# A decoder block on one core: first-stage elementwise work off GpSimd, merge products read from the bank, and new places for merge steps and last scalings

## The chip, the cores and the metric

The kernel runs on one core of a Trainium2 chip. A core has a matrix engine (TensorE; PE for matmuls, PEld for weight loads), VectorE (DVE), ScalarE (ACT), GpSimd (POOL) and SyncE (SP, which here only issues DMAs). Each engine works through its own instruction list in order and waits on semaphores. Matmul results land in eight PSUM banks of 128 x 512 float32, which DVE and ACT can read. The metric is the device time of one execution in microseconds (us), the median of three runs.

## The reference, cut to what matters

One layer, 1024 positions, width 1024, all float32:

```
h = rmsnorm(x);  z = h @ w_in;  gates = sigmoid(h @ w_gate + b_gate)     # 3 x 1024 gate columns
y_a = u * (chunked causal mix of layernorm(v))     # u, v = gelu of the first 512 columns of z
y_b = causal mean pooling (windows 2,4,8,16) of 256 columns, @ pool_w, * pool_scale
y_c = differential attention, 4 heads: softmax(q1 k1 + bias) - lam * softmax(q2 k2 + bias), @ v; rmsnorm per head
merged = g_a*(y_a @ proj_a) + g_b*(y_b @ proj_b) + g_c*(y_c @ proj_c)
x = x + merged @ w_out
x = x + (gelu(causal_conv(gate)) * up) @ w_down    # gate, up = rmsnorm(x) @ w_up, 2816 columns each
out = rmsnorm(x)
```

## The kernel before, in words

Activations are held transposed, features on the 128 partitions, eight tiles of 128 x 1024; j = 0, 1 are the two halves of 512 positions. Every float32 product is made of three matmuls of a rounded high part and a low remainder: ACT casts the high part, another engine subtracts it from the source to get the low part (the `split` lines, L96 and L97; L316 and L317 for h). The large products use a seven-product Strassen-like scheme (L189 holds all matmuls of it; `b` is a bank, T/S/A are combined operands).

**First stage** (to about 75 us). For j = 0 and then j = 1: x tiles are loaded, `scaled` makes the split h blocks (hb), 48 matmuls fill two banks `pu` (the u columns) and `v_part` two more per half (the v columns). `squares` (L330 on POOL for even tiles, L332 on ACT for odd) and the additions of L336 sum x² over the tiles; `factors` (L339 to L344) turns the sum into 1/rms, written to `R8` (R in the trace). `bcast_rows` (L146, L148) multiplies R into an identity on PE to spread it over partitions, and ACT copies the bank to `RB`, by which u is multiplied. After each half, `v_gelu` (L427) reads the v banks. `winograd` (L207 to L212) forms in place the combinations of x for the scheme, for tiles 0, 2 and 3 on POOL and for tile 1 on DVE. `load_V` loads the value weights in small parts through a pool of six half-size buffers (`wr`, in_w_tm) and splits them.

**Middle.** Values, the pooled columns (`pooling`, L542 to L551, woven into the first q/k product; `pool_out`, L576, its small product), q/k and 12 pairs of gate products; gates go to DRAM (g_d). `start` (L827, L830) copies a bank to an x tile with the residual added by DMA.

**Attention and merge** (about 460 to 660 us). 32 tiles of 128 queries run as a software pipeline over steps t. In a step, `scores` computes q k for the two softmaxes: chunk by chunk of up to 512 columns PE fills a bank, DVE adds the bias and takes the minimum of the negated scores in the same instruction (L675), a small DVE reduction joins the two chunks (L681), ACT takes the exponential (L683). `combine` (L1000 to L1002, DVE) subtracts the two softmaxes; `transpose` (PE L1017, ACT copy L1018) and `attend` (PE L1026, one bank) give the head's output, copied by ACT (L1029), whose squares DVE sums from SBUF (L1032). `sub_norm` (L1044 to L1056) normalizes a head. Between these pieces a generator `filler = merge_ab()` is advanced once per step: six matmuls into one of two `mm` banks, an ACT copy `pc` (L1096), a POOL multiplication by the gate tile (L1097), and after each fourth step a POOL addition of the b part to the a part (L1099). `load_p` loads and splits w_proj (low part on POOL for a/b, on DVE for c). `merge_c` multiplies the c part on DVE (L1122) and adds it to the same tile by an accumulating DMA issued from POOL (L104).

**End.** The last half of the last product is made in two quarters q (`tail2`): sums of squares on PE (L1287), 1/rms (`finish`, L1294 and L123 to L131), spreading (L1300), a copy to RB (L1303), and `scale_out` of four output pairs k: POOL after an ACT multiplication (L1251, L1252) or DVE in one instruction (L1254).

A scheduler orders the instructions of each engine from the program's order and its priorities; `tc.high_priority()` asks it to place what stands inside early. Buffers come from pools and are reused in order.

Of the kernel before, what the change touches and what calls it, by code (L numbers as in the profile page):

```python
# [15 lines left out]
ALU = mybir.AluOpType  # L16
# [31 lines left out]
def trunk_kernel(  # L48
# [147 lines left out]
    class Act:  # L196
# [2 lines left out]
            self.T = [{} for _ in range(4)]  # L199


        def winograd(self, xt, j, T4=True, eng=None):

            t, u = xt[j], xt[j + 4]
            b11, b12, b21, b22 = t[:, :NH], t[:, NH:], u[:, :NH], u[:, NH:]
            e = eng or nc.gpsimd
            e.tensor_tensor(out=b11, in0=b12, in1=b11, op=ALU.subtract)  # L207
            e.tensor_tensor(out=b12, in0=b22, in1=b12, op=ALU.subtract)
            e.tensor_tensor(out=b22, in0=b22, in1=b11, op=ALU.subtract)
            t1, t3 = op2(t, a4, "T")  # L210
            if T4:
                e.tensor_tensor(out=b21, in0=b21, in1=b22, op=ALU.subtract)  # L212
                t4, t2 = op2(u, a4, "T")
                self.T[j].update(T4=t4)
            else:
                t2 = op1(b22, "T2")
            self.T[j].update(T1=t1, T2=t2, T3=t3)
# [106 lines left out]
    def squares(kt, j):  # L324

        k = 2 * j + kt % 2
        src = xt[kt][:, half(j)]
        sq = c2("acc" if kt < 2 else "sq")
        if kt % 2 == 0:
            nc.gpsimd.tensor_tensor(out=sq, in0=src, in1=src, op=ALU.mult)  # L330
        else:
            nc.scalar.activation(out=sq, in_=src, func=AF.Square)  # L332
        if kt < 2:
            acc[k] = sq
        else:
            (nc.gpsimd, nc.vector)[kt % 2].tensor_tensor(out=acc[k], in0=acc[k], in1=sq, op=ALU.add)  # L336

    def factors(j):
        nc.vector.tensor_tensor(out=acc[2 * j], in0=acc[2 * j], in1=acc[2 * j + 1], op=ALU.add)  # L339
        ps = pm1()  # L340
        ss_cols(ps, acc[2 * j], 4, 1, 0)
        t = tiny(4, "ssum")
        nc.vector.tensor_scalar(out=t, in0=ps[:, :4], scalar1=1.0 / D, scalar2=1e-6, op0=ALU.mult, op1=ALU.add)
        nc.vector.tensor_copy(R8[:, 4 * j:4 * j + 4], rsqrt(t, 4, j == 0))  # L344

    def gain(kt):
        nc.scalar.mul(xt[kt], xt[kt], col(C_GA + kt))
# [87 lines left out]
    for j in range(2):  # L435
        pu = [pb1() for _ in range(2)]
        for kt in range(KT):
            if j == 0 and kt in (1, 2, 3):
                for g in gens:
                    next(g)  # L440
            if j == 0 and kt in (1, 3):
                for k in range(kt + 1, kt + 3):
                    load_x(k, 0)
                if kt == 3:
                    load_x(6, 0)
                    load_x(7, 0)
            if j == 0 and kt == 3:
                w_v = [next(load_parts(w_tm[0, k].rearrange("p a b -> p (a b)"), 1)) for k in range(2)]
            if j == 0 and kt == 5:
                for k in range(KT):  # L450
                    load_x(k, 1)
            if j == 0:
                scaled(kt, j)
            for i in range(2):
                mm3(pu[i], wsl(w_u[i], kt), h.b[kt][j], kt == 0, kt == KT - 1)
            if j == 1:
                squares(kt, 1)
        if j == 0:
            pv = [v_part(0, 0, lambda k: squares(k, 0))]
            factors(0)  # L460
            for kt in range(KT):
                scaled(kt, 1)
            pv.append(v_part(0, 1))
        else:
            w_V = [load_V(c) for c in range(2)]
            wk, wsm, pbd = load_wide()
            rel_bias()
            factors(1)
            pv = [v_part(1, 0)]
        bcast_rows(R8[:, 4 * j:4 * j + 4], 4, RB[:, half(j)], pm1)  # L470
        u_gelu(j, pu)
        if j == 1:
            pv.append(v_part(1, 1))
        for g in range(2):
            v_gelu(j, g, pv[g])
# [106 lines left out]
    h.winograd(xt, 0)  # L582
    layer_norm()
    values(1, (2, 3))
    h.winograd(xt, 1, eng=nc.vector)
    values(0, (0, 1))
    h.winograd(xt, 2)
    gating(0)
# [25 lines left out]
        store_qk(i, strassen_pair(ops, h, pb1, lambda: next(pl, None)))  # L614
    for _ in pl:
        pass
    for f in range(2):
        pool_out(f, zb[f])

    def load_head(hd):  # L620

# [30 lines left out]
    def scores(t, c):  # L652

        if t >= len(tiles):
            return
        hd, i = tiles[t]
        H = heads[hd]
        W = (i + 1) * P
        if c == 0:
            if W <= NH:  # L660
                b = a4([P, 2, NH], n="sc")
                st[t] = dict(pr=[b[:, 0, :], b[:, 1, :]], s=[])
            else:
                st[t] = dict(pr=[a4(n="sc"), a4(n="sc")], s=[])
        q, kh, kl = H["qkl"][c]
        sc_ = st[t]["pr"][c]
        mx = tiny(2, "mx")
        chunks = [(0, min(NH, W))] + ([(NH, W - NH)] if W > NH else [])
        for n_, (c0, n) in enumerate(chunks):
            ps = score_bank[0]()  # L670
            qs = q[:, i * P:(i + 1) * P]
            nc.tensor.matmul(ps[:, :n], lhsT=qs, rhs=kh[:, c0:c0 + n], start=True, stop=False)
            nc.tensor.matmul(ps[:, :n], lhsT=qs, rhs=kl[:, c0:c0 + n], start=False, stop=True)
            o = (7 - i) * P + c0
            nc.vector.tensor_tensor_reduce(  # L675
                out=sc_[:, c0:c0 + n], in0=ps[:, :n], in1=H["T"][:, o:o + n], scale=1.0, scalar=3.0e38,
                op0=ALU.add, op1=ALU.min, accum_out=mx[:, n_:n_ + 1])
        nm_ = mx[:, 0:1]
        if len(chunks) > 1:
            nm_ = tiny(1, "nmx")  # L680
            nc.vector.tensor_reduce(out=nm_, in_=mx, axis=AX.X, op=ALU.min)  # L681
        sum_ = H["s0"][:, i:i + 1] if c == 0 else tiny(1, "s1")
        nc.scalar.activation(out=sc_[:, :W], in_=sc_[:, :W], func=AF.Exp, bias=nm_, scale=-1.0, accum_out=sum_)  # L683
        st[t]["s"].append(sum_)

    for n_ in range(12):
        Fs = strassen_pair(w_gate[n_], h, pb1)
        for k, F in enumerate(Fs):
            m = 2 * n_ + k
            times_r(F)  # L690
            nc.scalar.activation(out=F, in_=F, func=AF.Sigmoid, bias=col(C_BG + m), scale=1.0)
            nc.sync.dma_start(out=g_d[m], in_=F)
# [31 lines left out]
    def strassen_full(src, w, nsl, x_d, out, done, tail=None, LL=4):  # L724
# [113 lines left out]
        def after(p):  # L838
            R4 = range(4)
            if p == 0:  # L840
                for d in R4:
                    later(1, start, d, 0, B[0][d])
            if p == 1:
                for d in R4:
                    plus(d, 0, B[1][d])
                for d in R4:
                    fin(d, 0, 3)
            if p == 2:
                for d in R4:
                    start(d, 1, B[0][d])  # L850
                for d in R4:
                    later(3, start, 4 + d, 1, B[2][d])
            if p == 3:
                for d in R4:
                    start(4 + d, 0, B[0][d])
                    later(4, plus, 4 + d, 1, B[0][d])
                for d in R4:
                    fin(4 + d, 1, 5)
            if p == 5:
                for d in R4:  # L860
                    plus(d, 1, B[2][d])
                    fin(d, 1, 5)
# [157 lines left out]
    def attend(t):  # L1020
# [4 lines left out]
        for kb in range(i + 1):  # L1025
            nc.tensor.matmul(po[:, :P], lhsT=AH[t][:, kb, :], rhs=H["V"][:, kb, :], start=kb == 0, stop=kb == i)  # L1026
            if kb % 4 == 3:
                yield
        nc.scalar.copy(H["O"][:, i, :], po[:, :P])  # L1029
        junk = c2("sq")  # L1030
        o = H["O"][:, i, :]
        nc.vector.tensor_tensor_reduce(out=junk[:, :P], in0=o, in1=o, scale=1.0, scalar=0.0, op0=ALU.mult,  # L1032
                                       op1=ALU.add, accum_out=H["ss"][:, i:i + 1])
        yield

    ycv = [[None, None] for _ in range(NHEAD)]
# [20 lines left out]
            ycv[hd][j] = op_g(pt, col(C_SG), "yc")  # L1057
            yield

    def load_p(m, g, eng=nc.gpsimd):  # L1060
        raw = c2(n="pr")
        nc.sync.dma_start(out=raw, in_=w_proj[m, :, 4 * g:4 * g + 4, :].rearrange("p a b -> p (a b)"))
        hl = w4([P, 2, NH], F32R, "ph")
# [21 lines left out]
    def merge_ab():  # L1085
        for m in range(KT):
            ga, gb, whl = ab(m)
            for j in range(2):
                if j == 1 and m < KT - 1:
                    ab(m + 1)  # L1090
                for g, k in ((ga, 0), (gb, 2)):
                    ps = pmm()
                    for ki in range(2):
                        mm3(ps, wsl(whl, k + ki), yab[k + ki][j], ki == 0, ki == 1)
                    t = c2("pc")
                    nc.scalar.copy(t, ps)  # L1096
                    nc.gpsimd.tensor_tensor(out=g[:, half(j)], in0=t, in1=g[:, half(j)], op=ALU.mult)  # L1097
                    if (g, j) == (gb, 1):
                        nc.gpsimd.tensor_tensor(out=ga, in0=ga, in1=gb, op=ALU.add)  # L1099
                        mg.append(ga)  # L1100
                    yield

# [27 lines left out]
    for t in range(len(tiles) + 3):  # L1130
# [10 lines left out]
            scores(t, 0)  # L1141
        transpose(t - 2, 0)
        next(avs, None)
        if t >= 1:
            next(filler, None)
        scores(t, 1)
        combine(t - 1)
# [9 lines left out]
            avs = attend(t - 2)  # L1157
        if lates and next(lates[0], 0) == 0:
            lates.pop(0)
        if t >= 29:  # L1160
            pre_c(t - 29)
        if t >= 34:
            next(mc)
    for _ in avs:
        pass
# [110 lines left out]
    def tail2(hold):  # L1276
# [13 lines left out]
        def finish(q):  # L1290
# [11 lines left out]
            sl = slice(q * n, (q + 1) * n)  # L1302
            nc.scalar.copy(RB[:, sl], pb[:, :n])  # L1303
            for k in range(4):
                scale_out(k, 0, sl, RB[:, sl], nc.gpsimd if k <= (2, 0)[q] else nc.vector)
            yield

        pend, fins = None, iter(())
# [143 lines left out]
```

## Time and profile before

| what | us |
|---|---|
| median of three runs (1421.44 to 1428.28) | 1421.71 |
| the profiled execution | 1421.06 |
| its span, first to last instruction | 1419.4 |
| PE busy | 1355.5 (96 %) |
| DVE busy | 984.9 (69 %) |
| ACT busy | 652.4 (46 %) |
| POOL busy | 621.7 (44 %) |

Busy time of PE is an upper measure, since matmuls are pipelined and their ends are modelled. [...]

### The profile page before, as it was taken

To read this page: it belongs to the slowest core of one execution; us is meant where nothing else is said; L and a number is where in the kernel's file an instruction comes from. 1 tells how busy PE (TensorE), PEld (TensorE's weight loads), DVE (VectorE), ACT (ScalarE), POOL (GpSimd) and SP (SyncE) were. 2 spreads that over 40 slices of the span, in tenths; PEclk is the share of its full clock that TensorE was granted. 3 is DMA by queue.
4 is the path that set the end of the run, shared out by engine and by line. 5 is a ranking of instruction groups with operands and counts; after the bars stand their busy time and mean duration, and the time that the engine had idled before them with its cause. 6 is when DMAs were issued, how large, how long until landed. Compare 5 with 4: busy or idle time off the path is not lost. (4 is left out here: it accounts for less than half of the span.)

```text
span 1419.4 us, 17845 instructions
## 1 busy us (share of the span) xinstructions
PE 1355.5 (96%) x6502; PEld 1130.4 (80%) x6502; DVE 984.9 (69%) x1502; ACT 652.4 (46%) x1065; POOL 621.7 (44%) x399
## 2 busy tenths in 40 slices
PE   7799999999999889989989999999999999999996
PEld 6699777888888677778868788888888887888786
DVE  8764676454444889976959766677676668985854
ACT  6442244443434666642567433343434335455461
POOL 6523365555544545442132466666666640102014
PEclk9999999999999999999999999999999999999998
DMA  5232044323336986358796122222222247945753
GB/s 188 96 112 90 30 178 151 132 104 119 120 118 173 287 223 185 105 185 191 185 245 159 52 102 77 90 89 74 90 89 74 75 144 273 305 128 151 215 127 119
DMA packets 78256, 200.46 MB, mean 141 GB/s; under 512 B 8206, under 2 KB 17550, under 8 KB 78168
## 3 DMA queue, kind: packets, MB, share of 16 engines
q1 hardware_dynamic: 67800, 180.44, 38.6%
q0 software_dynamic: 10368, 18.88, 7.9%
q8 instruction: 51, 0.84, 0.2%
q14 instruction: 37, 0.30, 0.1%
HBM read 143.70 MB, written 47.46 MB: 135 GB/s over the span
## 5 line engine op out<-in xcount | busy, mean ns | idle before, releaser
L189 PE MATMUL b<-ft,fw 128*128 128x512 f32 (+1 forms) x1308 | 291.7, 383 | 8.3 <-ACT ft L96 3.1
L189 PEld LDWEIGHTS b<-ft,fw 128*128 128x128 f32 x1308 | 238.9, 188 | 58.3 <-ACT ft L96 3.9
L351 POOL TENSOR_TENSOR F<-F,RB 128x1024 f32<-128x1024 f32 x74 | 206.0, 2785 | 145.9 <-DVE F L260 135.4
L189 PE MATMUL b<-hb,Ah 128*128 128x512 f32 x608 | 190.1, 392 | 0.0
L260 DVE TENSOR_TENSOR F<-b,c 128x512 f32<-128x512 f32 x152 | 100.8, 683 | 112.8 <-ACT c L279 68.7
L189 PE MATMUL b<-T,Sh 128*128 128x512 f32 x504 | 155.7, 389 | 1.9 <-ACT c L270 1.9
L232 POOL TENSOR_TENSOR s<-r 128x512 f32<-128x512 f32 x36 | 57.0, 1584 | 200.8 <-DMA r<-in_w_up 96.6
L189 PEld LDWEIGHTS b<-hb,Ah 128*128 128x128 f32 x608 | 114.5, 189 | 24.6 <-issue 1.0
L97 DVE TENSOR_TENSOR Sl<-s,Sh 128x1024 fp32r<-128x1024 f32 x76 | 114.0, 1500 | 26.2 <-PE b L189 22.1
L97 DVE TENSOR_TENSOR Al<-r,Ah 128x1024 fp32r<-128x1024 f32 x38 | 52.6, 1385 | 98.2 <-issue 77.7
L189 PE MATMUL b<-hb,Al 128*128 128x512 f32 x304 | 119.0, 392 | 0.8 <-DVE Al L97 0.8
L96 ACT CAST Sh<-s 128x1024 fp32r<-128x1024 f32 x76 | 80.0, 1052 | 72.8 <-PE b L189 48.6
L189 PEld LDWEIGHTS b<-T,Sh 128*128 128x128 f32 x504 | 94.6, 188 | 21.9 <-ACT c L270 2.4
L189 PE MATMUL b<-hb,Sh 128*128 128x512 f32 x304 | 95.4, 396 | 3.9 <-DVE F L260 3.9
L189 PE MATMUL b<-T,Sl 128*128 128x512 f32 x252 | 98.1, 389 | 0.0
L96 ACT CAST Ah<-r 128x1024 fp32r<-128x1024 f32 x38 | 40.0, 1053 | 110.4 <-PE b L189 106.7
L96 ACT CAST fw<-fr 128x512 fp32r<-128x512 f32 x90 | 54.7, 622 | 64.9 <-DVE fw L97 29.0
L189 PE MATMUL b<-Tl,Sh 128*128 128x512 f32 x204 | 79.4, 389 | 0.0
L189 PE MATMUL b<-Th,Sh 128*128 128x512 f32 x204 | 78.7, 390 | 0.7 <-ACT c L270 0.7
L189 PE MATMUL b<-Th,Sl 128*128 128x512 f32 x204 | 78.6, 389 | 0.0
L104 POOL DMA_DIRECT2D ssb<-sq x24 | 20.7, 876 | 125.8 <-ACT sq L171 37.8
L97 DVE TENSOR_TENSOR A<-r,A 128x512 fp32r<-128x512 f32 x38 | 74.6, 1964 | 0.9 <-ACT A L96 0.9
(260 smaller groups left out, 2982.8 us busy)
## 6 DMA issues: line engine op xcount, KB each, us to landing
fr<-in_w_down SPq DMA_DIRECT2D x47, 512.0 KB, 4.6
r<-in_w_up SPq DMA_DIRECT2D x42, 512.0 KB, 3.5
r<-in_w_gate SPq DMA_DIRECT2D x24, 512.0 KB, 4.1
g_d<-F SPq DMA_DIRECT2D x24, 512.0 KB, 4.8
act_d<-cv SPq DMA_DIRECT2D x22, 512.0 KB, 2.6
act<-act_d SPq DMA_DIRECT2D x22, 512.0 KB, 6.8
fr<-in_w_out SPq DMA_DIRECT2D x18, 512.0 KB, 4.0
ssb<-sq POOLq DMA_DIRECT2D x24, 256.0 KB, 3.9
```

Of the source, the lines that this page charges most:

```text
L96: nc.scalar.copy(hi, src)
L97: (eng or nc.vector).tensor_tensor(out=lo, in0=src, in1=hi.bitcast(F32), op=ALU.subtract)
L104: nc.gpsimd.dma_start(out=dst, in_=src, accum_op=ALU.add)
L189: nc.tensor.matmul(ps, lhsT=w[a], rhs=x[b], start=first and i == 0, stop=last and i == 2, skip_group_check=more)
L232: eng.tensor_tensor(out=s1[:, :NH], in0=a21, in1=a22, op=ALU.add)
L260: nc.vector.tensor_tensor(out=o, in0=ps, in1=c, op=ALU.add)
L351: (eng or nc.gpsimd).tensor_tensor(out=F, in0=F, in1=RB, op=ALU.mult)
```

## The change: what it does

- First stage: all squares go to ACT, all additions of squares and all of `winograd` to DVE; `factors` and the spreading of R stand under `high_priority`.
- `pool_out` is no longer called behind the q/k products but handed, through a generator, to the first gate products.
- `scores`: the second chunk's instruction takes the first chunk's minimum as its start value, so the reduction L681 goes.
- `attend`: the squares are taken on ACT from the bank, summed by the same instruction.
- `load_p` puts the low part on DVE for a/b too; in `merge_ab` DVE multiplies the bank by the gate tile in one instruction, and the addition of b to a becomes an accumulating DMA.
- The filler is left out at t = 10, 18, 26 and advanced twice from t = 32; `pre_c` and the advance of `merge_c` begin one step earlier.
- `start(d, 1, ...)` of the output products stands under `high_priority`.
- End: in quarter 0 POOL scales all four pairs; in quarter 1 POOL scales k = 0 and DVE scales the others with the bank itself as second input.

```
-        if kt % 2 == 0:
-            nc.gpsimd.tensor_tensor(out=sq, in0=src, in1=src, op=ALU.mult)
-        else:
-            nc.scalar.activation(out=sq, in_=src, func=AF.Square)
+        nc.scalar.activation(out=sq, in_=src, func=AF.Square)
...
-            (nc.gpsimd, nc.vector)[kt % 2].tensor_tensor(out=acc[k], in0=acc[k], in1=sq, op=ALU.add)
+            nc.vector.tensor_tensor(out=acc[k], in0=acc[k], in1=sq, op=ALU.add)
...
-        bcast_rows(R8[:, 4 * j:4 * j + 4], 4, RB[:, half(j)], pm1)
+        with tc.high_priority():
+            bcast_rows(R8[:, 4 * j:4 * j + 4], 4, RB[:, half(j)], pm1)
...
-                out=sc_[:, c0:c0 + n], in0=ps[:, :n], in1=H["T"][:, o:o + n], scale=1.0, scalar=3.0e38,
+                out=sc_[:, c0:c0 + n], in0=ps[:, :n], in1=H["T"][:, o:o + n], scale=1.0,
+                scalar=mx[:, 0:1] if n_ else 3.0e38,
...
-        nc.vector.tensor_tensor_reduce(out=junk[:, :P], in0=o, in1=o, scale=1.0, scalar=0.0, op0=ALU.mult,
-                                       op1=ALU.add, accum_out=H["ss"][:, i:i + 1])
+        nc.scalar.activation(out=junk[:, :P], in_=po[:, :P], func=AF.Square, accum_out=H["ss"][:, i:i + 1])
...
-                    t = c2("pc")
-                    nc.scalar.copy(t, ps)
-                    nc.gpsimd.tensor_tensor(out=g[:, half(j)], in0=t, in1=g[:, half(j)], op=ALU.mult)
+                    nc.vector.tensor_tensor(out=g[:, half(j)], in0=ps, in1=g[:, half(j)], op=ALU.mult)
                     if (g, j) == (gb, 1):
-                        nc.gpsimd.tensor_tensor(out=ga, in0=ga, in1=gb, op=ALU.add)
+                        accumulate(ga, gb)
...
-        if t >= 1:
+        if t >= 1 and t not in (10, 18, 26):
+            next(filler, None)
+        if t >= 32:
             next(filler, None)
...
-                scale_out(k, 0, sl, RB[:, sl], nc.gpsimd if k <= (2, 0)[q] else nc.vector)
+                if q == 0 or k == 0:
+                    scale_out(k, 0, sl, RB[:, sl], nc.gpsimd)
+                else:
+                    scale_out(k, 0, sl, pb[:, :n], nc.vector)
```

How the instructions move, at two places. First, DVE in the first stage, where R of the half j = 0 is finished: rs and ssum are the 128 x 4 values of the 1/rms computation, wl the low parts of the value weights, x the tiles that `winograd` combines. Before:

```order
37 L124 RECIPROCAL rs_48_326<-rs_49_327 128x4
38 L339 TENSOR_TENSOR acc_429<-acc_429,acc_437 128x512
39 L129 SCALAR_TENSOR_TENSOR rs_49_327<-rs_48_326 128x4
40 L130 TENSOR_TENSOR rs_49_327<-rs_49_327,ssum_324 128x4
41 L131 SCALAR_TENSOR_TENSOR rs_48_326<-rs_49_327,rs_48_326 128x4
42 L344 COPY R_93<-rs_48_326 128x4
43 L208 TENSOR_TENSOR x_86<-x_90,x_86 128x512
44 L97 TENSOR_TENSOR wl_494<-wr_495,wh_493 128x512
```

And in the changed kernel, from the third of these small instructions on:

```order
58 L131 SCALAR_TENSOR_TENSOR rs_48_326<-rs_49_327,rs_48_326 128x4
59 L97 TENSOR_TENSOR wl_494<-wr_499,wh_493 128x512
60 L209 TENSOR_TENSOR x_91<-x_91,x_87 128x512
61 L97 TENSOR_TENSOR wl_504<-wr_505,wh_503 128x512
62 L212 TENSOR_TENSOR x_90<-x_90 128x512
63 L97 TENSOR_TENSOR wl_504<-wr_509,wh_503 128x512
64 L209 TENSOR_TENSOR x_92<-x_92,x_88 128x512
65 L342 COPY R_93<-rs_48_326 128x4
```

The copy to R moves from row 42 to row 65, behind three splits of the value weights and most of the `winograd` instructions.

Second, PE at the same time: m_407 is the bank in which R is spread, b_421 and b_422 are the pu banks of j = 1, b_590 is the first v bank of j = 1. Before:

```order
159 L189 MATMUL b_421<-hb_343,wh_109 128x512 x2
160 L189 MATMUL b_421<-hb_343,wl_110 128x512
161 L189 MATMUL b_422<-hb_343,wh_115 128x512
162 L146 MATMUL m_407<-ident,R_93 128x128 x4
163 L189 MATMUL b_422<-hb_343,wh_115 128x512
164 L189 MATMUL b_422<-hb_343,wl_116 128x512
```

In the changed kernel:

```order
175 L189 MATMUL b_421<-hb_355,wh_109 128x512 x2
176 L189 MATMUL b_421<-hb_355,wl_110 128x512
177 L189 MATMUL b_422<-hb_355,wh_115 128x512 x2
178 L189 MATMUL b_422<-hb_355,wl_116 128x512
179 L146 MATMUL m_407<-ident,R_93 128x128 x4
180 L385 MATMUL m_547<-oh_544,rb 4x512
181 L189 MATMUL b_590<-wh_183,hb_334 128x256
```

The spreading of R now stands behind the last pu matmul (of hb_355, the eighth tile) and no longer behind those of the fourth tile (hb_343).

## Rows read from the trace of the kernel before

**Rows 1.** Busy time in stretches; PE, PEld, DVE, ACT, POOL (x instructions), PEclk, DMA share, GB/s.

```profile
0.00:20.00 20.00, 12.29 (x44) 8.82 (x45) 13.37 (x16) 15.19 (x28) 11.41 (x15) 0.88 0.85 290
...
40.00:60.00 20.00, 12.82 (x51) 10.47 (x50) 19.84 (x24) 8.45 (x14) 12.41 (x9) 0.83 0.31 103
...
460.00:500.00 40.00, 34.90 (x188) 28.22 (x187) 31.41 (x87) 25.26 (x55) 19.38 (x11) 0.96 0.97 280
500.00:540.00 40.00, 36.41 (x223) 31.97 (x222) 34.41 (x116) 26.38 (x68) 18.61 (x12) 0.96 0.77 214
540.00:580.00 40.00, 37.42 (x233) 31.93 (x233) 37.31 (x133) 28.29 (x72) 18.87 (x14) 1.00 0.62 172
580.00:635.00 55.00, 45.95 (x265) 38.86 (x264) 44.95 (x139) 31.36 (x79) 24.03 (x17) 0.94 0.43 137
```

**Rows 2.** PE in the first stage, in order of time: start, duration, instruction, idle before.

```profile
18.27 0.79 PE L189 MATMUL b<-hb,wh 128*128 128x512 f32 x1 [4.67 <-DVE hb L317]
51.19 2.05 PE L146 MATMUL m<-ident,R 128*128 128x128 f32 x8 [7.18 <-DVE R L344]
61.54 0.38 PE L189 MATMUL b<-wh,hb 128*128 128x256 f32 x1
```

**Rows 3.** DVE, then ACT, in the first stage, in order of time.

```profile
24.05 0.68 DVE L336 TENSOR_TENSOR acc<-acc,sq 128x512 f32<-128x512 f32 x1
...
44.28 0.17 DVE L124 RECIPROCAL rs<-rs 128x4 f32<-128x4 f32 x1
...
49.85 1.19 DVE L344 COPY R<-rs 128x4 f32<-128x4 f32 x1
...
55.97 0.62 ACT L96 CAST wh<-wr 128x512 fp32r<-128x512 f32 x1 [6.63 <-DMA wr<-in_w_tm]
57.09 1.28 ACT L427 ACT_TABLE_LOAD   x1
58.39 1.57 ACT L427 ACTIVATE vg<-b,R 128x256 f32<-128x256 f32 x4
```

**Rows 4.** PE at the small pooling product, in order of time.

```profile
167.69 2.81 PE L576 MATMUL m<-F,wpp 128*128 128x512 f32 x4 [2.61 <-issue]
```

**Rows 5.** What PE waited for, 460 to 635 us: total us, times, longest.

```profile
PE sc L672 <- DVE mx L675: 5.5, 4, 2.6
...
PE b L189 <- DVE F L260: 1.4, 1, 1.4
```

**Rows 6.** Groups of DVE and ACT instructions, 460 to 640 us: busy, mean ns, idle before.

```profile
L1032 DVE CUSTOM_DVE_ANT_0 sq<-O 128x128 f32<-128x128 f32 x32 | 17.0, 533 | 5.3 <-ACT O L1029 5.3
L1001 DVE SCALAR_TENSOR_TENSOR nr<-nr,s,nlam 128x1 f32<-128x1 f32 x32 | 12.8, 401 | 0.6
L1002 DVE SCALAR_TENSOR_TENSOR sc<-sc,nr,sc 128x896 f32<-128x896 f32 x4 | 6.6, 1646 | 0.1
L681 DVE TENSOR_REDUCE nmx<-mx 128x1 f32<-128x2 f32 x32 | 4.7, 148 | 0.1
...
L1096 ACT COPY pc<-mm 128x512 f32<-128x512 f32 x32 | 18.4, 583 | 3.9 <-PE mm L189 3.9
```

**Rows 7.** DVE and POOL at two places of the attention, in order of time.

```profile
590.16 1.15 DVE L1002 SCALAR_TENSOR_TENSOR sc<-sc,nr,sc 128x896 f32<-128x896 f32 x1
...
615.31 1.24 DVE L1044 TENSOR_TENSOR e<-s 128x4 f32<-128x4 f32 x1
...
615.14 1.39 POOL L1097 TENSOR_TENSOR gb<-pc,gb 128x512 f32<-128x512 f32 x1 [3.14 <-ACT pc L1096]
```

**Rows 8.** The page: a group of DVE instructions that read a bank.

```profile
L260 DVE TENSOR_TENSOR F<-b,c 128x512 f32<-128x512 f32 x152 | 100.8, 683 | 112.8 <-ACT c L279 68.7
```

**Rows 9.** The page: accumulating DMAs issued from POOL, KB each, us to landing.

```profile
ssb<-sq POOLq DMA_DIRECT2D x24, 256.0 KB, 3.9
```

**Rows 10.** DVE at the end, in order of time.

```profile
1406.58 0.41 DVE L1324 TENSOR_TENSOR x<-b,x 128x256 f32<-128x256 f32 x1
...
1412.05 3.49 DVE L1254 SCALAR_TENSOR_TENSOR x<-x,cs,RB 128x256 f32<-128x256 f32 x6 [1.72 <-ACT RB L1303]
```

More of the change, by code (lines that the diff above doesn't have):

```diff
@@ L199, in __init__, with winograd @@
             self.T = [{} for _ in range(4)]
-        def winograd(self, xt, j, T4=True, eng=None):
+        def winograd(self, xt, j, T4=True):
             t, u = xt[j], xt[j + 4]
             b11, b12, b21, b22 = t[:, :NH], t[:, NH:], u[:, :NH], u[:, NH:]
-            e = eng or nc.gpsimd
+            e = nc.vector
             e.tensor_tensor(out=b11, in0=b12, in1=b11, op=ALU.subtract)
@@ L335, in squares @@
         else:
-            (nc.gpsimd, nc.vector)[kt % 2].tensor_tensor(out=acc[k], in0=acc[k], in1=sq, op=ALU.add)
+            nc.vector.tensor_tensor(out=acc[k], in0=acc[k], in1=sq, op=ALU.add)
     def factors(j):
[L339 to L344, printed above, removed]
+        with tc.high_priority():
+            nc.vector.tensor_tensor(out=acc[2 * j], in0=acc[2 * j], in1=acc[2 * j + 1], op=ALU.add)
+            ps = pm1()
+            ss_cols(ps, acc[2 * j], 4, 1, 0)
+            t = tiny(4, "ssum")
+            nc.vector.tensor_scalar(out=t, in0=ps[:, :4], scalar1=1.0 / D, scalar2=1e-6, op0=ALU.mult, op1=ALU.add)
+            nc.vector.tensor_copy(R8[:, 4 * j:4 * j + 4], rsqrt(t, 4, j == 0))
     def gain(kt):
@@ L469, in trunk_kernel @@
             pv = [v_part(1, 0)]
-        bcast_rows(R8[:, 4 * j:4 * j + 4], 4, RB[:, half(j)], pm1)
+        with tc.high_priority():
+            bcast_rows(R8[:, 4 * j:4 * j + 4], 4, RB[:, half(j)], pm1)
         u_gelu(j, pu)
@@ L584, in trunk_kernel @@
     values(1, (2, 3))
-    h.winograd(xt, 1, eng=nc.vector)
+    h.winograd(xt, 1)
     values(0, (0, 1))
@@ L616, in trunk_kernel, with pool_outs @@
         pass
-    for f in range(2):
-        pool_out(f, zb[f])
+    def pool_outs():
+        for f in range(2):
+            for _ in range(2):
+                yield
+            pool_out(f, zb[f])
+    po_ = pool_outs()
     def load_head(hd):
@@ L675, in scores @@
             nc.vector.tensor_tensor_reduce(
-                out=sc_[:, c0:c0 + n], in0=ps[:, :n], in1=H["T"][:, o:o + n], scale=1.0, scalar=3.0e38,
+                out=sc_[:, c0:c0 + n], in0=ps[:, :n], in1=H["T"][:, o:o + n], scale=1.0,
+                scalar=mx[:, 0:1] if n_ else 3.0e38,
                 op0=ALU.add, op1=ALU.min, accum_out=mx[:, n_:n_ + 1])
[L678 to L681, printed above, removed]
+        nm_ = mx[:, n_:n_ + 1]
         sum_ = H["s0"][:, i:i + 1] if c == 0 else tiny(1, "s1")
@@ L686, in trunk_kernel @@
     for n_ in range(12):
-        Fs = strassen_pair(w_gate[n_], h, pb1)
+        Fs = strassen_pair(w_gate[n_], h, pb1, lambda: next(po_, None))
         for k, F in enumerate(Fs):
@@ L849, in after @@
                 for d in R4:
-                    start(d, 1, B[0][d])
+                    with tc.high_priority():
+                        start(d, 1, B[0][d])
                 for d in R4:
@@ L1030, in attend @@
         junk = c2("sq")
-        o = H["O"][:, i, :]
-        nc.vector.tensor_tensor_reduce(out=junk[:, :P], in0=o, in1=o, scale=1.0, scalar=0.0, op0=ALU.mult,
-                                       op1=ALU.add, accum_out=H["ss"][:, i:i + 1])
+        nc.scalar.activation(out=junk[:, :P], in_=po[:, :P], func=AF.Square, accum_out=H["ss"][:, i:i + 1])
         yield
@@ L1058, in sub_norm, with load_p @@
             yield
-    def load_p(m, g, eng=nc.gpsimd):
+    def load_p(m, g, eng=nc.vector):
         raw = c2(n="pr")
@@ L1159, in trunk_kernel @@
             lates.pop(0)
-        if t >= 29:
-            pre_c(t - 29)
-        if t >= 34:
+        if t >= 28:
+            pre_c(t - 28)
+        if t >= 33:
             next(mc)
```

## The prediction

> **What bounds the kernel now.** I read the page's busy shares first: PE 96 %, the next engine 69 %, so only time in which PE stands still or runs slowly can be won. The view by stretches shows where that is. From 0 to 20 and from 40 to 60 us PE is busy 12 to 13 us of 20, the granted clock averages 0.88 and 0.83, and DVE is busy 19.84 of 20 in the second; from 460 to 635 PE is busy 155 of 175 us, the clock 0.96, 0.96, 1.00 and 0.94, DVE 148 [rows 1]. The rest of the program has few gaps. PE's order of time then names the waits: 4.67 us on the split of h and 7.18 us on R in the first stage, both on DVE [rows 2]. In the attention seven entries of the view of waits name DVE as what PE waited for, from 5.5 down to 1.4 us, 18.1 in all; the first and last are in [rows 5]. DVE itself is slowed. A 512-wide addition takes 0.68 us and a 128x4 instruction 0.17 when nothing runs on POOL; the four small instructions that finish R while POOL works on x take about 1.2 each [rows 3], and a 128x4 square in the attention takes 1.24 beside a POOL multiplication of 1.39 [rows 7]. So work on POOL is paid for by DVE.
>
> **First stage.** Removed from POOL: eight squares (to ACT), six additions and twelve `winograd` instructions (to DVE). DVE gets 18 instructions of some 0.65, 12 us, and loses the stretching. What PE loses there before: 4.67 + 7.18 of waits, and half clock for 20 x (1 - 0.88) / 0.5 = 4.8 us and 20 x (1 - 0.83) / 0.5 = 6.8 us, nearly 12 us, of which the two waits cover some 5; the rest runs at half speed, which costs half of it, 3.2. Smaller waits add 1. Together 16.
> Against this stands a new wait. The copy to R is now behind splits and `winograd` (DVE row 65 instead of 42). Between the eight hb of j = 1 and that copy the order has about 32 instructions of 512 columns; at 0.62 from start to start that is 20 us, from about 25 us (where the wide splits of j = 0's weights end, earlier than before since the hb group is not stretched): R is ready at 45.4. PE would reach the first v part of j = 1 (b_590) at 61.54 - 16 = 45.5 [rows 2] if nothing new held it. It is held: the copy to RB stands behind all eight casts of the value weights on ACT (before behind six), and summing ACT's list the last cast ends at about 46.6. Then RB copy 0.6, the table load 1.28 and two gelus at 0.4 [rows 3], and only then is the bank free that this v part takes: 49.3. The difference to 61.54 is 12.2; I take a stretch of half clock behind the new wait of 4 us at 1.2 and forecast -11. Bounds: the copies wait for the last part of the value weights, whose arrival ended a 6.63 us wait of ACT at 55.97 [rows 3]; if it comes no earlier than 51 the gain is 6. If the bank comes as PE ends, it is 13. `high_priority` on R and its spreading brings neither forward in the order; it is not counted.
>
> **Pooling.** Of the pooled columns' product only the second tile's two matmuls move into the gate products; the first tile's stay where PE waits 2.61 [rows 4] for a chain on DVE that is not shortened. I count -0.5, between 0 and -2.6 (all of that wait).
>
> **Attention.** DVE loses 32 squares (17.0) and 32 reductions (4.7) [rows 6], 21.7. It gets 32 multiplications that read a bank, at the 0.68 of the nearest such group [rows 8], 22, and eight splits at 0.69, 5.5: +27.5. That is 6 more, before the stretching goes. POOL's work here, 19.38 + 18.61 + 18.87 + 24.03 = 81 us [rows 1], all but goes. Of what remains on DVE, the 32 small scalings of L1001 take 0.40 each where a small one takes 0.17 to 0.22: 6 us; the 896-wide subtractions 1.65 in the mean against 1.15 of an undisturbed one [rows 6, 7]: 0.5 for each of 32, some 14 at most since the narrow ones lose less; the small ones of `sub_norm` a few more. I take 22 of relief, so DVE falls by some 16 of 148, 11 %. ACT loses 32 copies of 0.58 [rows 6] and gets 32 narrow squares that cost less than such a copy each: no loss.
> What can it give? The ceiling is 18.1 of waits on DVE and half of the half-clock time (13 us by the clocks of [rows 1]), 6.5: some 25. With 11 % off an engine that is 85 to 93 % busy I let half of the waits go, 9, and half of the clock loss, 3; against it I set 2 for the accumulating DMAs, 4 MB more where the DMA share is 0.97 [rows 1]. Result -10. Bounds: -20 (nearly the ceiling) and +4 (each multiplication now waits at the head of DVE's list for its six matmuls and for the gate tile, and the score additions, for which PE waits, are queued behind; the one `ms` bank is held for the square after the copy).
> The added DMAs land 3.9 us after issue in the nearest row (256 KB) [rows 9]; each new one is 512 KB, so some 4 to 8, and only the last lies near the end of the stage. [...]
> `start` of the second half stands at the same place of ACT's list in spite of its priority: 0.
>
> **End.** Before, the six scalings of the last quarter on DVE took 3.49 from 1412.05, after a copy of 0.4; now they read the bank at the 0.41 of a 256-wide instruction from PSUM [rows 10] without the copy: 0.4 + 3.49 - 6 x 0.42 = 1.4 less. Two DVE scalings of quarter 0 that delayed the addition at 1406.58 go: 0.9. Against it POOL works two instructions longer (1.5) while the small 1/rms instructions run, which may stretch three of them by 0.5. Together -1 (from -2.4 to +0.8).
>
> **Sum.** -11 - 0.5 - 10 - 1 = -22.5 against the profiled execution of 1421.06, so 1398.6; the median lies 0.65 above that execution, so 1399.
>
> **Rivals.**
> (a) Only the first stage pays. DVE takes on 27.5 us, its waits on banks and tiles replace the stretching, and PE's waits in the attention stay. For it: DVE stays the busiest engine beside PE, at some 132 of 175. Against: nothing in the rows is longer than before but the waits. 1399 + 10 = 1409.
> (b) The first stage's gain is eaten: R and the RB copy wait for the value weights, whose loads need buffers that DVE frees late. For it: the 6.63 us wait in [rows 3], and the copy to R behind three such splits. Against: the splits that free them come earlier too. -3 instead of -11: 1407.
> (c) Slower. The multiplications stall DVE: each is in its list before its six matmuls (1.5 us by PE's rate) are done. If each waits for the whole of them, 32 x 1.5 = 48 us of stall less the 16 won is +32 on the engine that bounds the stage, of which, since PE works meanwhile, some two thirds would show: +21, with the other stages -12.5: 1430. It decides from a mean stall of about 1.1 us per multiplication. Against it: ACT's copies at the same place waited 3.9 us for PE in all 32 [rows 6].
> (d) The change doesn't do what it says: the moved instructions come out where the same waits hold them (as `start` and the first pooled tile do). 1420.
>
> **How the numbers follow.** Forecast 0.55, (a) 0.21, (b) 0.10, (c) 0.07, (d) 0.07. The forecast's own bounds reach from 1386 to 1409. The range takes in (a) and (b) and leaves (c) and (d) out: 1385 to 1414. What a measurement here can tell from no change is 0.5 %, 7 us: faster are nearly all of the forecast, (a) and (b), 0.84; within 0.5 % (d) and what (a) leaves, 0.09; slower 0.07.
>
> **What would show it.** Right: PE's wait for hb at 18 us gone; the spreading of R without a 7 us wait, one wait of about 4 us ahead of the first v part of j = 1, which starts near 49; small DVE instructions at 0.17 there and in the attention; DVE near 132 us between 450 and 620; PE's wait at the pooling product unchanged, and the x copies of `start` as before. Wrong: the v part not before 55; PE's waits on DVE in the attention still 15 us or more; idle time on DVE ahead of L1097 of over 15 us; a wait of PE for the merged tiles at the end of the stage.

## The result, and the profile after

| | before | after |
|---|---|---|
| median, us (four runs each, same chip) | 1421.58 | 1400.15 (1398.53 to 1402.35) |
| ratio | | 0.9839, 95 % interval 0.9807 to 0.9871 |
| profiled execution, us | 1421.06 | 1398.53 |
| its span | 1419.4 | 1396.8 |
| PE / DVE / ACT / POOL busy | 1355.5 / 984.9 / 652.4 / 621.7 | 1349.3 / 954.8 / 647.7 / 517.9 |

The change makes the kernel 1.6 % faster. 1399 was forecast, with a range from 1385 to 1414.

Where the time came from is best seen as PE's loss: over all matmuls, the interval to the next one's start less the median interval of its width (0.227 us for 512 columns, 0.120 for 256, 0.111 for 128), summed by stretch. It is worked out from the start times of the trace; the medians add up to 1320.9 us in both kernels, so the same work is done and only the loss moves.

| stretch, us | loss before | loss after | difference | forecast |
|---|---|---|---|---|
| first stage, 0 to 80 | 23.5 | 11.4 | -12.1 | -11 |
| values to gates, 80 to 440 | 11.5 | 10.9 | -0.6 | -0.5 |
| attention and merge, 440 to 640 | 32.5 | 24.9 | -7.6 | -10 |
| output product, 640 to 800 | 8.6 | 8.9 | +0.3 | 0 |
| 800 to the last matmul | 13.0 | 11.1 | -1.9 | -1 |

The sum is -21.9; the span fell by 22.6, the rest lying behind the last matmul. Each loss is read from one execution.

First stage, PE in order of time, after (the rows that answer to [rows 2]: start, duration, instruction, idle before):

```profile
13.25 1.54 PE L189 MATMUL b<-hb,wh 128*128 128x512 f32 x3 [1.78 <-ACT hb L316]
...
45.52 1.05 PE L146 MATMUL m<-ident,R 128*128 128x128 f32 x8
...
49.40 0.39 PE L189 MATMUL b<-wh,hb 128*128 128x256 f32 x1 [1.88 <-ACT vg L425]
```

The two long waits on DVE are gone, the spreading of R does not wait, and the v part b_590 starts at 49.40 instead of 61.54, behind a wait for its bank that ends with the gelu. DVE and ACT in the same stretch (to [rows 3]):

```profile
38.84 0.15 DVE L131 SCALAR_TENSOR_TENSOR rs<-rs,rs 128x4 f32<-128x4 f32 x1
38.91 0.68 DVE L97 TENSOR_TENSOR wl<-wr,wh 128x512 fp32r<-128x512 f32 x1
...
42.52 0.16 DVE L342 COPY R<-rs 128x4 f32<-128x4 f32 x1
...
45.04 1.14 ACT L96 CAST wh<-wr 128x512 fp32r<-128x512 f32 x2 [5.30 <-PE b L189]
46.61 0.59 ACT L148 COPY RB<-m 128x512 f32<-128x512 f32 x1 [0.43 <-PE m L146]
47.22 1.28 ACT L425 ACT_TABLE_LOAD   x1
```

Every DVE instruction shown has its undisturbed duration (0.17 and 0.68 in [rows 3]), and R is ready at 42.7 although 23 more instructions stand ahead of it. The copy to RB stands behind the last casts, as forecast, but these wait for PE's last pu matmuls, not for the transfer, and they end at 46.2: what the copy itself waits for, 0.43 us, is the spreading on PE.

Attention, by stretches (columns as in [rows 1]; PEclk is the granted clock of TensorE as a share of the full one); the first 65 us and the rest:

```profile
445.00:510.00 65.00, 54.31 (x284) 44.62 (x283) 45.38 (x129) 36.71 (x91) 6.97 (x6) 0.92 0.95 263
510.00:620.00 110.00, 106.95 (x655) 92.11 (x654) 94.78 (x307) 71.02 (x214) 7.67 (x9) 1.00 0.80 208
```

From 510 on PE is busy 97 % of the time at full clock (granted 1.00); DVE has room (86 %). Before, the same part of the stage ran at 93.6 % (540 to 580) and 83.5 % (580 to 635) [rows 1]. The first 65 us have become no better, and there the DMA share is 0.95. What PE waits for, 445 to 620 us (to [rows 5]):

```profile
PE mm L189 <- ACT ph L96: 3.8, 2, 2.6
PE at L1021 <- DVE sc L1006: 2.7, 4, 1.5
PE sc L677 <- DVE mx L680: 2.2, 3, 1.6
...
PE mm L189 <- DVE ga L1097: 1.3, 1, 1.3
```

The waits on the score additions fell from 5.5 to 2.2. The largest is now the one on the cast of w_proj, which was 0.9 before; the longer of its two waits, 2.6, is at the end of a transfer. Groups of DVE and ACT, 445 to 632 us (to [rows 6]):

```profile
L1097 DVE TENSOR_TENSOR gb<-mm,gb 128x512 f32<-128x512 f32 x16 | 11.0, 687 | 5.6 <-DMA gb<-g_d 1.9 <-PE mm L189 1.9 <-DMA pr<-in_w_proj 1.6
L1097 DVE TENSOR_TENSOR ga<-mm,ga 128x512 f32<-128x512 f32 x16 | 11.0, 685 | 4.2 <-DMA ga<-g_d 2.7 <-PE mm L189 1.3
...
L1005 DVE SCALAR_TENSOR_TENSOR nr<-nr,s,nlam 128x1 f32<-128x1 f32 x32 | 6.9, 217 | 0.5
...
L1035 ACT ACTIVATE sq<-ms 128x128 f32<-128x128 f32 x32 | 9.2, 286 | 0.0
...
L1035 ACT ACTIVATION_READ_ACCUMULATOR sq<-ms 128x1 f32 x32 | 6.6, 208 | 0.0
```

The added multiplications take 0.686 as taken from [rows 8]; L1005, the old L1001, fell from 0.401 to 0.217; DVE stood idle 9.8 us ahead of all 32 multiplications, 0.3 each.

### The profile page after: what moved, and what is told of

The parts are those of the page before. It is cut to its first block, busy times and chain, and to the rows that moved or that the text cites. A ratio compares the mean times of both kernels' runs of the same rounds, so it can differ in the third digit from the quotient of the medians.

```text
span 1396.8 us, 17805 instructions
## 1 busy us (share of the span) xinstructions
PE 1349.3 (97%) x6502; PEld 1126.9 (81%) x6502; DVE 954.8 (68%) x1462; ACT 647.7 (46%) x1107; POOL 517.9 (37%) x335
## 5 line engine op out<-in xcount | busy, mean ns | idle before, releaser
L97 DVE TENSOR_TENSOR Sl<-s,Sh 128x1024 fp32r<-128x1024 f32 x76 | 120.2, 1582 | 29.0 <-ACT Sh L96 19.8
L97 DVE TENSOR_TENSOR Al<-r,Ah 128x1024 fp32r<-128x1024 f32 x38 | 50.5, 1330 | 103.5 <-issue 76.4
L189 PE MATMUL b<-wh,hb 128*128 128x256 f32 x384 | 71.9, 286 | 1.9 <-ACT vg L425 1.9
L189 PEld LDWEIGHTS b<-hb,Sh 128*128 128x128 f32 x304 | 56.9, 188 | 16.2 <-DVE F L260 4.4
```

What stands on the lines that cost most here:

```text
L97: (eng or nc.vector).tensor_tensor(out=lo, in0=src, in1=hi.bitcast(F32), op=ALU.subtract)
L189: nc.tensor.matmul(ps, lhsT=w[a], rhs=x[b], start=first and i == 0, stop=last and i == 2, skip_group_check=more)
```

## The experiments

Each was timed in five rounds against the kernel before on its chip; the ratio stands with its 95 % interval. The changed kernel's ratio is 0.9839 (0.9807 to 0.9871), so a difference of 0.01 in ratio is 14 us and two kernels are told apart from some 0.004. Losses are PE's, worked out as above, with the same intervals for every kernel. Each comes from the one profiled execution, which can lie anywhere among a kernel's executions (in u_merge it is the slowest of 12, 1417.53, in u_sched the fastest of six, 1395.3), so 2 or 3 us in one stage are weak evidence by themselves.

**First stage put back** (u_first). The edits of `squares`, `winograd`, `factors` and `bcast_rows` undone, as

```
-            e = nc.vector
+            e = eng or nc.gpsimd
```

> The changed kernel with its first stage put back (squares, their additions and the combinations of x on GpSimd as before, no priority); the rest stays changed. Theory (all of the first stage's gain comes from these lines): 12 us slower than the changed kernel, about 1412, the first v part of the second half at about 61.5 us again. Rival (part of it came from later stages that start in another DMA state): 6 to 9 slower.

Measured: 1415.04, ratio 0.9963 (0.9948 to 0.9978). The loss from 0 to 80 us is 23.5 again (11.4 after), in every other stretch within about 1 us of the changed kernel. So the first stage's gain is its own: 12.1 by the trace; the ratios say 18, give or take 5.

**Useless work on GpSimd in the first stage** (d_first). No useful instruction is moved.

```
+    on4 = ones.unsqueeze(1).broadcast_to([P, 4, P])
+    for _ in range(36):
+        nc.gpsimd.tensor_tensor(out=vg[1]..., in0=on4, in1=on4, op=ALU.mult)
```

> The changed kernel with 36 useless 512-wide multiplications on GpSimd from the start of the program, results in a tile that is overwritten later; every useful instruction stays on its engine. GpSimd is then busy from about 1 to 45 us. Theory (work on GpSimd stretches VectorE): VectorE's 512-wide additions take 1.2 to 1.8 instead of 0.68, R is ready 4 to 8 us later, the kernel 4 to 9 us slower. Rival (the gain came from which engine does what and from the order, not from GpSimd being idle): no change within 1.5 us.

Measured: 1420.84, ratio 1.0005 (0.9988 to 1.0021): the whole gain of the change is gone. DVE, POOL and PE of this kernel in order of time:

```profile
1.33 45.25 POOL L375 TENSOR_TENSOR vg<-ones 128x512 f32<-128x512 f32 x33
```

```profile
34.42 2.06 DVE L97 TENSOR_TENSOR wl<-wr,wh 128x1024 fp32r<-128x1024 f32 x1
...
44.16 1.52 DVE L333 TENSOR_TENSOR acc<-acc,sq 128x512 f32<-128x512 f32 x1
45.61 1.52 DVE L317 SCALAR_TENSOR_TENSOR hb<-x,cs,hb 128x512 fp32r<-128x512 f32 x1
47.06 0.68 DVE L333 TENSOR_TENSOR acc<-acc,sq 128x512 f32<-128x512 f32 x1
...
64.63 0.16 DVE L342 COPY R<-rs 128x4 f32<-128x4 f32 x1
```

```profile
24.43 0.80 PE L189 MATMUL b<-hb,wh 128*128 128x512 f32 x1 [8.84 <-DVE hb L317]
```

POOL works without a pause until 46.6, and up to there the same DVE addition takes 1.52, from there on 0.68. R is ready 22 us later than in the changed kernel, the loss from 0 to 80 us is 32.6 instead of 11.4: +21.2, the whole difference of the spans (+20.3). The mechanism is shown; its size was underestimated, since the useless work is denser than the old GpSimd work was.

**Attention put back** (u_att): merge products, squares, reduction and places of the merge steps as before (the edits of u_merge, u_sqmin and u_sched below, together).

> The changed kernel with the attention part put back (merge products by a ScalarE copy and GpSimd, GpSimd addition, low parts on GpSimd, squares and the joining reduction on VectorE, the old places of the merge steps). Theory: 7 to 10 us slower than the changed kernel, about 1408, PE's gaps from 520 us on come back. Rival (the attention gave nothing, the rest is the first stage and the boundary between stages): within 3 us.

Measured: 1407.16, ratio 0.9915 (0.9899 to 0.9931). Loss from 440 to 640 us 32.6 (24.9 after, 32.5 before). The theory holds: 8 us by the trace, 11 give or take 5 by the ratios.

**Merge products alone put back** (u_merge), with the low parts of w_proj on GpSimd again.

```
+                    t = c2("pc")
+                    nc.scalar.copy(t, ps)
+                    nc.gpsimd.tensor_tensor(out=g[:, half(j)], in0=t, in1=g[:, half(j)], op=ALU.mult)
...
+                        nc.gpsimd.tensor_tensor(out=ga, in0=ga, in1=gb, op=ALU.add)
```

> The changed kernel with only the merge products put back (ScalarE copy, GpSimd multiplication, GpSimd addition of b to a, GpSimd low parts). Theory (GpSimd's 75 us of work stretch VectorE, this is the whole of the attention's gain): 7 to 10 us slower than the changed kernel, L1005 back from 0.22 to 0.40 us. Rival (squares, reduction and the places of the merge steps carry it): 0 to 3 slower.

Measured: 1412.16, ratio 0.9937 (0.9917 to 0.9957), 14 us slower than the changed kernel, give or take 5. Loss from 440 to 640 us 34.8, 640 to 800 13.3. The small scaling is slower than in the kernel before (0.401), DVE in the groups view of this kernel:

```profile
L1005 DVE SCALAR_TENSOR_TENSOR nr<-nr,s,nlam 128x1 f32<-128x1 f32 x32 | 14.4, 450 | 0.7
```

So this part carries the attention's gain, as the theory had it, and without it the other parts are worth nothing. It puts back two things at once, 78 us of GpSimd work and the longer chain over ScalarE; d_att2 below adds GpSimd work alone.

**Squares and reduction alone put back** (u_sqmin).

```
-                scalar=mx[:, 0:1] if n_ else 3.0e38,
+                scalar=3.0e38,      # and the tensor_reduce behind it
-        nc.scalar.activation(out=junk[:, :P], in_=po[:, :P], func=AF.Square, accum_out=...)
+        nc.vector.tensor_tensor_reduce(out=junk[:, :P], in0=o, in1=o, ..., accum_out=...)
```

> The changed kernel with the squares and the joining reduction back on VectorE: it gets 64 instructions with their reads of the sum, about 32 x 0.28 + 32 x 0.08 + 32 x 0.15 = 16 us where nothing on GpSimd disturbs. Theory: VectorE is no longer the bound, so 2 to 4 us slower. Rival (VectorE still bounds the stage): 8 or more.

Measured: 1402.39, ratio 0.9867 (0.9837 to 0.9897); the interval overlaps the changed kernel's. Loss from 440 to 640 us 27.8, +2.9. Some 16 us more on DVE cost PE 3: with GpSimd nearly silent DVE sets the pace far less.

**Places of the merge steps put back** (u_sched), with `pre_c` and `merge_c` one step later again.

```
-        if t >= 1 and t not in (10, 18, 26):
+        if t >= 1:
             next(filler, None)
-        if t >= 32:
-            next(filler, None)
```

> The changed kernel with the merge steps at their old places (one per step from t = 1, no doubling, the third product one step later). Theory (the places only fill the last tiles): 1 to 3 us slower, the gaps between 590 and 615 us come back in part. Rival (they matter as much as the silence of GpSimd): 5 or more.

Measured: 1400.62, ratio 0.9849 (0.9818 to 0.9881): no difference; the loss from 440 to 640 us is 24.8. My 1 to 3 us were wrong. From 510 us to the end of the stage PE lost 5.5 us with the old places (7.0 in the changed kernel), and 17.9 in u_att, which has the old places too but GpSimd's work beside them: the gaps in the last query tiles came with that work and not from missing merge work.

**Addition of b to a back on GpSimd** (u_add).

```
-                        accumulate(ga, gb)
+                        nc.gpsimd.tensor_tensor(out=ga, in0=ga, in1=gb, op=ALU.add)
```

> The changed kernel with the addition of b to a back on GpSimd (8 x 2.4 us) in place of the accumulating DMAs (4 MB). What is asked: whether the DMAs hurt the crowded start of the attention (DMA share 0.9, each landed 11 us after issue). If DMA bounds it: 1 to 4 us faster than the changed kernel. If GpSimd's silence is worth more: 1 to 3 us slower.

Measured: 1407.7, ratio 0.9895 (0.9863 to 0.9927), 8 us slower, give or take 6. So 20 us of GpSimd additions cost more than the accumulating DMAs. But these are not free: from 445 to 510 us, where the DMA share is 0.95, PE loses 14.1 us without them and 18.0 with them. What GpSimd's additions cost comes behind that: 13.0 instead of 7.0 from 510 to 640, and 14.4 instead of 8.9 from 640 to 800 us, where the merged tiles are used. Why so much lands there is not settled.

**Useless work on GpSimd in the attention** (d_att, d_att2). In the first, behind each merge product, a GpSimd multiplication into a small buffer; in the second, behind 28 of the 32, into a dead half of RB. The edit of the second:

```
+                    if m >= 1:
+                        gg = g[:, half(j)]
+                        nc.gpsimd.tensor_tensor(out=RB[:, :NH], in0=gg, in1=gg, op=ALU.mult)
```

> The changed kernel with one useless 512-wide GpSimd multiplication behind each of the 32 merge products (reads the product, writes a scratch buffer). GpSimd gets about 42 us of work in the attention, VectorE keeps its instructions. Theory (the gain is GpSimd's silence): VectorE's small instructions go back to 0.4 to 1.2 us in part, PE loses 4 to 8 us, about 1405 to 1408. Rival (the gain is the shorter chain: no ScalarE copy, no reduction, squares elsewhere): within 2 us of the changed kernel.

> As d_att, but the useless GpSimd multiplications (28 of 512 columns, behind the merge products of all tiles but the first) write a dead half of RB, so no small buffer is taken from the pool through which w_proj is loaded, and the other engines' order stays nearer to the changed kernel's. Theory (GpSimd's work beside VectorE costs): 3 to 9 us slower than the changed kernel, L1005 at 0.3 to 0.4. Rival (the 17 us of d_att came from the buffers it took): within 2 us.

Measured: 1417.7, ratio 0.9989 (0.9971 to 1.0007), and 1412.17, ratio 0.9949 (0.9926 to 0.9973): 21 and 16 us slower, both more than expected. In d_att the loss from 440 to 640 us is 39.1; there the buffers of the pool through which w_proj comes are taken too, so I read d_att2, whose useless work takes 32 us of GpSimd. DVE in the attention of d_att2:

```profile
L97 DVE TENSOR_TENSOR ph<-pr,ph 128x512 fp32r<-128x512 f32 x16 | 11.6, 736 | 0.4 <-ACT ph L96 0.4
...
L1097 DVE TENSOR_TENSOR gb<-mm,gb 128x512 f32<-128x512 f32 x16 | 11.0, 686 | 8.2 <-PE mm L189 6.3 <-DMA gb<-g_d 1.7
...
L1005 DVE SCALAR_TENSOR_TENSOR nr<-nr,s,nlam 128x1 f32<-128x1 f32 x32 | 9.9, 310 | 0.4
```

L1005 is at 0.31 as expected (0.217 in the changed kernel). The split of w_proj (L97), with both inputs in SBUF, takes 0.736 instead of 0.686, while the merge products, one of whose inputs is a bank, stay at 0.686. The stage lost 4.9 us more than in the changed kernel (29.8 to 24.9 from 440 to 640 us), within the 3 to 9 expected, and all of it behind 510 us (13.1 instead of 7.0). So GpSimd's work alone, with no useful instruction moved to another engine, costs PE time in this stage. Another 7.7 came from 640 to 800 and 3 behind that, where the kernel is unchanged. In these kernels the b-to-a accumulation also stands behind the useless work in POOL's list, and the order of the other engines moved somewhat, so the whole 16 us are not a clean price of the contention.

**Value weights loaded later** (i_lv): `load_V` called behind the last u and v parts.

```
-            w_V = [load_V(c) for c in range(2)]
...
             pv.append(v_part(1, 1))
+            w_V = [load_V(c) for c in range(2)]
```

> The changed kernel with the loading and splitting of the value weights called behind the last u and v parts of the first stage, so that ScalarE's copy to RB stands ahead of all their casts. Theory (the new wait of 2 us ahead of b_590 is the casts'): the wait goes, 1.5 to 2.5 us faster, b_590 near 47.3. Rival (the value weights come late then): PE waits for them near 62 us and it is the same or up to 4 us slower.

Measured: 1410.05, ratio 0.9933 (0.9911 to 0.9955), 13 us slower, give or take 5. The rival is right in kind, though its wait comes later and costs more than it said. The bank wait went (the v part in the place of b_590 started at 47.97), and a longer one on the casts of the value weights came; PE in order of time:

```profile
47.97 0.39 PE L189 MATMUL b<-wh,hb 128*128 128x256 f32 x1 [0.45 <-DVE uT L409]
74.31 0.80 PE L189 MATMUL b<-wh,hb 128*128 128x256 f32 x2 [6.82 <-ACT wh L96]
```

But the wait did not go for the theory's reason. ACT's copy to RB, with no cast ahead of it, in the same kernel:

```profile
46.60 0.58 ACT L148 COPY RB<-m 128x512 f32<-128x512 f32 x1 [9.12 <-PE m L146]
```

It starts when it did in the changed kernel (46.61), released by the same spreading on PE. The casts had held nothing; the v part now takes a bank that DVE's `uT` frees (0.45 us of wait) and no longer one that the gelu frees.

**The same with later merge steps** (i_lvfill): from t = 4, doubled from t = 30.

```
-        if t >= 1 and t not in (10, 18, 26):
+        if t >= 4 and t not in (10, 18, 26):
             next(filler, None)
-        if t >= 32:
+        if t >= 30:
```

> i_lv with the merge steps started at t = 4 instead of 1 and advanced twice from t = 30. Theory (the first third of the attention is bound by DMA, share 0.9): 2 to 5 us faster than i_lv, PE's losses from 445 to 515 down from 18 us. Rival (the work is only shifted into the last tiles, where gaps come back): within 2 us of i_lv.

Measured: 1421.02, ratio 1.0000 (0.9983 to 1.0016), 10 us slower than i_lv. The loss from 440 to 640 us rose from 25.7 to 27.8, and one wait of 9.0 us on the c products (L1122) came at 662 us: the merged tiles are late for the output product. Neither is right: the losses from 445 to 515 went up (18.7 to 21.6), and the shift does not cost gaps in the last query tiles but the handover to the next stage.

**Half of the value weights later, gate tiles and w_proj asked for earlier** (i_best).

```
-            w_V = [load_V(c) for c in range(2)]
+            w_V = [load_V(0)]
...
+            w_V.append(load_V(1))
             pv.append(v_part(1, 1))
...
-                if j == 1 and m < KT - 1:
-                    ab(m + 1)
                 for g, k in ((ga, 0), (gb, 2)):
+                    if j == 0 and k == 2 and m < KT - 1:
+                        ab(m + 1)
```

> The changed kernel with only the second half of the value weights loaded behind the u and v parts (so that four casts, not eight, stand ahead of the copy to RB, and the first half still comes early), and the gate tiles and w_proj of the next merge tile asked for two products earlier. Theory (2 us of bank wait in the first stage; 5 us of waits on w_proj and gate tiles in the crowded first third of the attention): 2 to 5 us faster than the changed kernel, b_590 near 48. Rival (DMA is full there, an earlier request only moves another transfer back; late value weights): the same within 2 us, or slower by up to 5.

Measured: 1406.78, ratio 0.9907 (0.9885 to 0.993), 10 us slower, give or take 6; its profiled execution is 3 us longer than the changed kernel's. Both aims were met where they were set: b_590's place starts at 46.91 with 0.45 us of wait, the loss from 0 to 80 us is 8.9 (11.4), the waits on the cast of w_proj fell from 3.8 to 0.8. But 3.3 us of waits on the loads of the keys (kh, kl) came in their place, which the changed kernel does not have: as the rival had it, the earlier requests moved another transfer back. From 640 to 800 us the loss rose from 8.9 to 15.0. PE in order of time there:

```profile
650.06 17.98 PE L189 MATMUL b<-ft,fw 128*128 128x512 f32 x78 [2.89 <-DVE gc L1123]
669.68 0.49 PE L189 MATMUL b<-ft,fw 128*128 128x512 f32 x1 [1.65 <-ACT ft L96]
```

No version tried beats the changed kernel; u_sched and u_sqmin cannot be told from it.

## Why the prediction was right

**First stage.** The time of b_590 was forecast at 49.3 and measured at 49.40, and R's delay behind 23 more instructions did not matter: it was ready at 42.7, and forecast at 45.4. That GpSimd's work is what DVE paid for was argued from [rows 3]; d_first shows it, by the same instructions at 1.52 and 0.68.

One link came at the right time by another cause. The working let the eight casts hold the copy to RB until 46.6. They ended at 46.2, and the copy, at 46.61, waited for the spreading of R, which PE does behind its last pu matmul; i_lv, without the casts, has the copy at 46.60. That the two ends lie 0.4 us apart is luck. The new wait in front of the bank, forecast at 4 us, measured 1.9, because PE got there 2 us later than 45.5: its loss in the first 20 us fell only from 11.4 to 8.0. The longest wait left there, 1.78 us ahead of 13.25, is for a cast of h on ACT, which had idled 0.25 us for x until 11.96 (DMA share 0.86) and then made one of its new squares (0.63) first. Half clock is a granted clock of 0.50, as from 49.2 to 56.0 us in the kernel before: there the eight matmuls that spread R took 2.05 us [rows 2], at 1.00 in the changed kernel 1.05. No half clock followed the shorter wait at the bank (granted 1.00 from 40 to 60 us).

**Pooling.** PE's wait stays, 2.66 (2.61 in [rows 4]), as the order said. That the stretch from 80 to 440 us gained 0.6, where 0.5 was forecast, is luck: the half clock behind this wait went (granted 1.00 in the 15 us around it, 0.89 before), which gave 1.6, and the wait for a split of DVE (Al) shortly behind it grew from 0.8 to 2.5.

**Attention.** The direction and the mechanism held: u_merge shows that the gain hangs on the merge work's leaving GpSimd, and d_att2 that GpSimd's work alone brings back 4.9 us of loss. How much of the rest is the longer chain over ScalarE is not shown. Part by part, PE's waits on DVE fell from 18.1 to 9.0, just the half that the working let go. The half clock of the stage fell only from some 14 us to 10, worth 1.7 where 3 was taken. The mis-sized term is the deduction of 2 for the accumulating DMAs: the waits on the cast of w_proj alone grew by 2.9, and u_add, without these DMAs, loses 14.1 from 445 to 510 where the changed kernel loses 18.0, so some 4.

That is the first 65 us. From 510 to 640 the loss is 7.0 us (before, 520 to 640, 19.3), more than half of what could be had. From 445 to 510 PE lost 18.0 against 13.2 before (460 to 520): there the DMA share is 0.95, and the new accumulates took 11.3 us to land (the first two; 7.6 in the median for the next six) where I had put 4 to 8. No run tells whether full DMA engines made them late. The granted clock was 0.92 in the mean there.

One sign came out otherwise: DVE was to be busy near 132 us between 450 and 620, and was for 139.9. In the stretch that holds the same matmul work as 460 to 635 before (447.6 to 615.1) it is 137.6 against 148.1, 10.5 us less and not 16. Some 2 us of the difference are the second chunk's instruction, which takes the first's minimum: 0.749 us for 512 columns where the first takes 0.683.

**End.** -1 forecast, -1.1 found, and by the terms of the forecast. The two scalings no longer delay the last addition: from PE's last half-width group but one to the reduction of the sums of squares 5.6 us before (from 1402.79) and 4.5 after (from 1380.90). The six scalings got 1.05 us shorter, but they still begin only when ACT's copy to RB ends. Against it the small 1/rms instructions were stretched beside POOL, so that from that reduction to the spreading on PE 2.0 us became 3.0:

```profile
1387.08 0.65 DVE L130 TENSOR_TENSOR rs<-rs,ssum 128x2 f32<-128x2 f32 x1
...
1390.13 2.44 DVE L1256 SCALAR_TENSOR_TENSOR x<-x,cs,b 128x256 f32<-128x256 f32 x6 [1.72 <-ACT RB L1305]
```

The 1.9 us in the last line of the table are not this gain, most of which lies behind the last matmul. They lie between the up and the down product, where PE's wait on DVE is 2.2 us instead of 2.5 and no half-clock stretch follows it (before, 3.4 us at 0.50 from 1185.8). No term of the forecast had them.

**The rivals.** (a) is out: the attention gave 8 us. (b) is out: the weights' transfers came earlier with the splits that free their buffers; the last casts, started at 45.04, wait for PE and no longer for a transfer (6.63 us until 55.97 before [rows 3]). (c): DVE stood idle 0.3 us ahead of a merge product in the mean, far from the 1.1 at which it decides. (d): true of `start` (PE waits 1.5 us for its copy at 695.5 us) and of the first pooled tile, not of the rest.

**Open.** From 640 to 800 us the loss is between 7.1 and 18.7 us in the kernels tried, though none of these edits is there. Earlier or later merged tiles, and waits on the c products (9.0 us in i_lvfill), are part of it. So is the clock: some 10 us of this stretch are at half clock in u_add and d_att2 and some 14 in d_att and i_lvfill, against 3.4 in the changed kernel. But u_merge loses 13.3 us there with none. No run separates the causes.

## What to carry to other kernels

Where GpSimd and VectorE both work on SBUF tiles and VectorE feeds the bound engine, put GpSimd's work on VectorE's bill: here a 512-wide addition on VectorE took 1.52 us while GpSimd worked and 0.68 behind that work (d_first), and giving VectorE more instructions and GpSimd few shortened VectorE's list from 984.9 to 954.8 us. Useless work on the suspected engine, with every other instruction in place, is a good test of such a contention, if it takes no buffer and stands ahead of nothing useful in that engine's list. A time that comes out as forecast does not show the link that was forecast: the casts of the value weights show how two links can end together. A wait won in one stage is only a gain if the next handover keeps it: here two repairs that removed the waits they aimed at made the whole slower.

## What the runs showed of the hardware that I had not expected

In d_first the stretching did not grow with the width of the instruction: as long as GpSimd works without a pause (its own instruction 1.37), an addition of 512 columns takes 1.52 us and the first one behind that work 0.68; a split of 1024 columns takes 2.06 instead of the changed kernel's 1.22. Both are 0.84 longer. The merge products, with a bank as one input, kept 0.686 in d_att2, and the 512-wide score instructions, which read a bank too, took 0.684 in the kernel before, beside 81 us of GpSimd work, and 0.683 in the changed one. Executions of one kernel in these experiments differ by more (1402 to 1417 us in d_att2, 1395 to 1404 in u_sched) than the four runs of the changed kernel (1398.5 to 1402.4), so differences below some 5 us are not told by the times, and by a trace only where one of its rows explains them.
